# RG-LRU gates placed one by one among the products of a later projection, in a hybrid RG-LRU / latent-attention layer

## The chip, the core and the metric

The kernel runs on one core of a Trainium2 chip. TensorE (PE) multiplies matrices into PSUM, VectorE (DVE) and ScalarE (ACT) work on what it leaves there, GpSimd (POOL) takes elementwise work, and the queue of SyncE (SP) issues the DMAs. Each engine takes its instructions in order and waits at an instruction until the semaphores that it names are high enough. The metric is the device time in microseconds, as the median of several runs. Before the change it is 1305.29 us (three runs, 1304.16 to 1306.97).

## What is computed

One layer of a diffusion backbone: 1024 latent tokens and 256 context tokens of width 1024. This is the part of the reference that the change touches:

```python
xr_l, gr_l, cq_l, ckv_l, kr_l = split_in_proj(h_lat @ w_in)       # and the same for h_ctx
xcv_l = dwconv(xr_l, lru_conv_w, lru_conv_b, LRU_CONV_LEFT)        # 4 taps along the tokens
...
r = sigmoid(einsum('blhi,hij->blhj', xh, w_a) + b_a)               # 8 heads of 64
i = sigmoid(einsum('blhi,hij->blhj', xh, w_x) + b_x)
log_a = -LRU_C * r * softplus(-lam)
a = exp(log_a)
u = sqrt(-expm1(2 * log_a)) * (i * xc)                             # h_t = a_t h_(t-1) + u_t, both directions
...
y_lru_l = (lat_states[0] + lat_states[1]) * gelu(gr_l)
```

Beside it stand the modulation vectors silu(c) @ w_mod, the latent attention (its keys and values come from ckv), the output projection and a gated convolutional FFN.

## The kernel before

The program has five parts, one behind the other: a first part that loads and normalises the tokens and projects the token-major columns; the eight feature-major projections, with the RG-LRU between them; the start of the attention (values, keys, queries); the attention; the output projection and the FFN. The change is in the second part alone.

There, `proj` makes one block of 128 columns of `w_in` at a time. Every product is done as three fp32r products (high x high, high x low, low x high), over eight slices k of the contraction, into one PSUM tile with the tag "big" (name pf). Blocks 0 to 3 are the inputs of the convolution and cover all 1280 tokens (72 products), blocks 4 to 7 are the gelu branch and cover 1024 (48 products). `conv(m, po)` has ScalarE copy the block out of PSUM twice, VectorE adds the taps, and two DMAs write the halves of 64 rows, exchanged, into a page of their own (`xcs`). `gate(m, d, g)` makes one of the four gates of block m (two directions, a and x) from `xc` and `xcs`: six fp32 products in 64x64 tiles of the array, into another "big" tile (name pg), and a sigmoid on ScalarE that empties it. The tag "big" has two buffers, which the projections and the gates share; a product into a third tile waits until one of the two has been read. `coefs` (Exp, Tanh and the product with xc) and `scans` (Sqrt, then two scans in each direction on VectorE) follow. The table `after = {1: 0, 2: 1, 3: 2, 5: 3}` says behind which projection the four gates, coefs and scans of block m are written; for block 3 `tok_norm` and `ckv_t` (ten transposes of ckv into tiles with the tag "sm", names ck) come behind its coefs, and its scans one projection later.

The sixteen modulation steps (`mod2_step`) also stand between the projections, three or two at a time. Each takes two pages of `w_mod` (512 KB each, DMAs on SyncE's queue) and issues four fp32 products of 32 columns, two for each page (j) and half (h), each in its own quarter of the array, into a tile with the tag "sm" (name pm). Every fourth step ends a vector: ScalarE copies it out, and four small products or one wide one bring it into its place (the last goes through VectorE and two small DMAs for each half of the row). The tag "sm" has two buffers as well, shared by pm and ck. The pages of `R()` are twelve, used by w_mod, xr, xc, xcs, gates and coefficients in turn.

Inside the second part a scheduler of the framework sets the order of each engine's instructions, from the order in which the program is written and from an estimate of when operands are ready; `tc.issue_after(x)` holds what is issued inside its block behind x. The first part, the attention and the FFN are ordered by hand; the scheduler also orders the start of the attention.

Of the kernel before, what the change touches and what calls it, by code (L numbers as in the profile page):

```python
# [34 lines left out]
def hybrid_layer_kernel(ctx: ExitStack, tc: tile.TileContext, A, out):  # L35
# [20 lines left out]
    def R(dt=F32, shape=(128, 1280)):  # L56
        cnt[0] += 1
        return rp.tile(list(shape), dt, tag="R", name=f"r{cnt[0]}")
# [343 lines left out]
    acc2 = {}  # L402
# [10 lines left out]
    def mod2_step(s):  # L413

        n, kp = divmod(s, 4)
        if s + 1 < 16:
            mod2_load(s + 1)
        if kp == 0:
            acc2[n] = ps_small()
        ws_ = w2.pop(s)  # L420
        for j in range(2):
            for h in range(2):
                g = 64 * h + 32 * j
                T.matmul(acc2[n][g:g + 32, :], cs[:, 2 * kp + j, :], ws_[j][:, h * 512:(h + 1) * 512], start=kp == 0, stop=kp == 3,
                         tile_position=(0, g))
        if kp == 3:
            mr = R()
            S.activation(mr[:, 0:512], acc2.pop(n), AF.Copy)
            po = ps_small()
            if n < 2:  # L430
                pt = po[:, 0:8].rearrange("p (m h) -> p m h", h=2)
                for m in range(4):
                    T.matmul(pt[:, m, :], mr[:, m * 128:(m + 1) * 128], sel2, start=True, stop=True)
                V.tensor_copy(mod2[:, n].rearrange("p (h m) -> p m h", h=2), pt)
            else:
                T.matmul(po[0:2, :], sel2, mr[:, 0:512], start=True, stop=True)
                r = 2 * (n - 2)
                rw, gr = (mr[0:2, 512 + 256 * x:768 + 256 * x] for x in range(2))
                for h in range(2):
                    c = slice(h * 256, (h + 1) * 256)  # L440
                    for x, q_ in ((rw, r), (gr, r + 1)):
                        nc.sync.dma_start(out=x, in_=A["rows"][q_:q_ + 1, :].rearrange("o (a b) -> (o a) b", a=2)[:, c])
                    V.tensor_tensor(rw, po[0:2, c], rw, ALU.add)
                    V.tensor_tensor(rw, rw, gr, ALU.mult)
                    nc.sync.dma_start(out=gt_d[n - 2:n - 1, :].rearrange("o (a b) -> (o a) b", a=2)[:, c], in_=rw)
# [36 lines left out]
        split(raw, hi, lw, eh, el)  # L482
        return hi, lw

    def proj(w, chunks, name):

        hi, lw = w
        po = ps1.tile([128, 1536], F32, tag="big", name=name, bufs=2)
        for k in range(8):
# [4 lines left out]
                T.matmul(po[:, t0:t0 + n], wh, h_rng(hlo, k, t0, n), start=False, stop=False)  # L494
            for t0, n in chunks:
                T.matmul(po[:, t0:t0 + n], wl, h_rng(hhi, k, t0, n), start=False, stop=(k == 7))
        return po


# [33 lines left out]
    def conv(m, po):  # L533
# [9 lines left out]
                V.scalar_tensor_tensor(out=x[:, a:b], in0=xr[:, a + d:b + d], scalar=cw[k], in1=x[:, a:b],  # L543
                                       op0=ALU.mult, op1=ALU.add)

        y = xcs[m] = R()
        for p in (0, 64):
            nc.sync.dma_start(out=y[64 - p:128 - p, :], in_=x[p:p + 64, :])

# [22 lines left out]
        S.activation(g[:, :SEQ], po[:, :SEQ], AF.Gelu_apprx_tanh)  # L572
        V.tensor_tensor(ysum[m], ysum[m], g[:, :SEQ], ALU.mult)

    def gates(m):
        return [(gate(m, d, 0), gate(m, d, 1)) for d in range(2)]

    def coefs(m, ri):

        au = []  # L580
        for d in range(2):
            r, i = ri[d]
            c = slice(d * 4 + m, d * 4 + m + 1)
            a = R()
            S.activation(a, r, AF.Exp, scale=n8[:, c])
# [83 lines left out]
        return ps1.tile([128, 512], F32, tag="sm", name=f"pm{cnt[0]}", bufs=2)  # L669

    order = list(range(8))
    after = {1: 0, 2: 1, 3: 2, 5: 3}
    ws = prep_w(load_w(A["w_fm"][0]), "a", "v")
    raw = load_w(A["w_fm"][1])
    STEPS2 = [range(3 * n, 3 * n + 3) if n < 4 else range(12 + 2 * (n - 4), 14 + 2 * (n - 4)) if n < 6 else () for n in range(8)]
    with tc.issue_after(last_x.ins), tc.issue_after(last_h.ins):
        mod2_load(0)
    for n, m in enumerate(order):
        po = proj(ws, CH3 if m < 4 else CH3[:2], f"pf{m}")
        if n < 7:  # L680
            ws = prep_w(raw, "a", "v")
            if n < 6:
# [5 lines left out]
            conv(m, po)  # L688
        else:
            gated(m - 4, po)  # L690
        if m in after:
            au = coefs(after[m], gates(after[m]))
            if m == 5:
                tok_norm()
                ckv_t()
                au3 = au
            else:
                scans(after[m], au)
        if m == 6:
            raw = load_w(A["w_ukv"])  # L700
            wkh, wkl = prep_w(raw, "a", "v")
            scans(3, au3)
    pe_ctx.close()
    pe_ctx = ExitStack()
    ps2 = pe_ctx.enter_context(tc.tile_pool(name="ps2", bufs=4, space=PSUM, reuse_waits="tile"))
# [1072 lines left out]
```

## Time and profile before

| what | value |
|---|---|
| median of three runs | 1305.29 us (1304.16 to 1306.97) |
| the profiled execution | 1307.54 us |
| its span, first to last instruction | 1305.7 us |
| busy: PE / DVE / ACT / POOL | 97% / 78% / 56% / 30% |
| PE idle, all waits together | about 40 us of the span |
| second part (the projections) on PE | 90 to 247 us |
| mean granted clock of TensorE | 0.99 |

A busy share is an average over the whole span. The chain of waits follows the last instruction back to what released it, step by step; a share of it is time that set the end. In a timeline a row gives the start, the duration, the engine, the source line, the operation, and what it writes and reads; in brackets stands how long the engine was idle before it and who released it. Line numbers in these rows are those of the kernel before.

### The profile page before, as it was taken

The numbers are of one execution on the slowest core, as the hardware profiler recorded it, in microseconds if no ns is written. First come the engines' busy times: TensorE is split into PE (matmuls) and PEld (weight loads), VectorE is DVE, ScalarE is ACT, GpSimd is POOL, SyncE is SP. The second block draws the span as 40 slices with busy tenths as digits, with TensorE's granted clock in tenths as the row PEclk, the third lists the DMA queues.
The fourth block names the chain that finished last, engine by engine and source line by source line (L and its number), as shares of the span: only waits on it lengthen the run. The fifth ranks groups of instructions, "written<-read, shape, count | busy, mean of one in ns | idle before, by whom it ended". The sixth has DMA issues, their size and how long they took to land.

```text
span 1305.7 us, 18162 instructions
## 1 busy us (share of the span) xinstructions
PE 1265.6 (97%) x6586; PEld 1042.3 (80%) x6586; DVE 1012.0 (78%) x1665; ACT 735.5 (56%) x1376; POOL 388.9 (30%) x366
## 2 busy tenths in 40 slices
PE   5999999899999999999998999999999999999997
PEld 2796665687999999888877888888888888888886
DVE  3653677767888888857579888777877878897798
ACT  4543885557999999953375334433442343434581
POOL 2410000225666666733100443244234320000013
PEclk9999999999999999999998999999999999999999
DMA  9534463000000001243422222221222149205043
GB/s 371 206 102 149 128 193 124 13 1 2 2 1 2 2 1 30 86 162 113 146 80 97 83 83 77 97 97 67 79 97 81 66 141 365 90 1 177 1 146 129
DMA packets 45737, 126.85 MB, mean 97 GB/s; under 512 B 9016, under 2 KB 9296, under 8 KB 45648
## 3 DMA queue, kind: packets, MB, share of 16 engines
q1 hardware_dynamic: 45648, 125.69, 27.9%
q8 instruction: 52, 0.85, 0.3%
q14 instruction: 37, 0.30, 0.1%
HBM read 101.02 MB, written 22.03 MB: 94 GB/s over the span
## 4 chain that ended last, share of the span: by engine, by line
PE 81%; DVE 10%; ACT 4%; DMA 3%; issue 2%; SPq 0%; DVEq 0%; POOL 0%; ACTq 0%; POOLq 0%
PE b L1240 10%; PE b L1238 10%; PE b L1239 10%; PE t L937 5%; PE po L1086 4%; PE b L1415 4%; PE b L1416 4%; PE b L1414 4%; PE o L961 3%; PE o L962 3%; PE s L901 3%; PE s L902 3%; PE s L903 3%; DVE l L76 2%; PE po L1089 2%; PE pf L492 2%
## 5 line engine op out<-in xcount | busy, mean ns | idle before, releaser
L1240 PE MATMUL b<-l,f 128*128 128x512 f32 x620 | 242.6, 391 | 2.2 <-DVE f L76 2.2
L1238 PE MATMUL b<-l,f 128*128 128x512 f32 x620 | 242.5, 391 | 1.9 <-ACT f L1213 1.4
L1239 PE MATMUL b<-l,f 128*128 128x512 f32 x620 | 242.4, 391 | 0.9 <-DVE l L76 0.9
L1240 PEld LDWEIGHTS b<-l,f 128*128 128x128 f32 x620 | 117.1, 189 | 27.2 <-DVE f L76 3.0
L1238 PEld LDWEIGHTS b<-l,f 128*128 128x128 f32 x620 | 117.1, 189 | 26.7 <-ACT f L1213 1.9
L1239 PEld LDWEIGHTS b<-l,f 128*128 128x128 f32 x620 | 117.0, 189 | 26.1 <-DVE l L76 1.7
L1213 ACT ACTIVATE f<-w 128x1024 fp32r<-128x1024 f32 x21 | 22.3, 1060 | 201.9 <-POOL w L1210 193.6
L929 POOL TENSOR_SCALAR r<-r,c 128x512 f32<-128x512 f32 (+1 forms) x128 | 100.8, 799 | 97.9 <-DVE c L924 55.0
L906 DVE TENSOR_REDUCE c<-s 128x1 f32<-128x512 f32 (+1 forms) x192 | 108.7, 594 | 26.1 <-PE s L903 24.5
L76 DVE TENSOR_TENSOR f<-w,f 128x1024 fp32r<-128x1024 f32 (+1 forms) x90 | 98.4, 1095 | 34.1 <-ACT f L1213 33.1
L1297 DVE SCALAR_TENSOR_TENSOR l<-f,c,l 128x1023 f32<-128x1023 f32 x88 | 121.5, 1381 | 0.7
L917 ACT ACTIVATE r<-s,c 128x512 f32<-128x512 f32 (+1 forms) x192 | 117.5, 620 | 6.3 <-DVE c L924 4.8
L1207 POOL TENSOR_TENSOR w<-w 128x512 f32<-128x512 f32 x19 | 24.5, 1288 | 300.9 <-DVE f L76 300.9
L76 DVE TENSOR_TENSOR l<-t,l 128x512 fp32r<-128x512 f32 x128 | 81.5, 679 | 1.5 <-ACT l L69 1.3
L937 PE MATMUL t<-c,r 128*128 128x128 f32 x640 | 81.7, 273 | 0.9 <-DVE r L76 0.6
L69 ACT ACTIVATE l<-t 128x512 fp32r<-128x512 f32 x128 | 69.4, 595 | 8.8 <-PE t L937 7.9
L937 PEld LDWEIGHTS t<-c,r 128*128 128x128 f32 x640 | 71.3, 140 | 2.6 <-PE t L937 0.8
L1291 ACT ACTIVATE l<-f,c 128x1024 f32<-128x1024 f32 x44 | 54.4, 1237 | 31.7 <-DVE f L1278 31.2
L1637 POOL TENSOR_TENSOR f<-f,w 128x1024 f32<-128x1024 f32 (+1 forms) x5 | 11.7, 2376 | 202.7 <-ACT l L1603 202.7
L901 PE MATMUL s<-r,w 96*128 96x512 f32 (+1 forms) x192 | 69.5, 362 | 1.0 <-ACT r L917 0.7
L1086 PE MATMUL po<-l,r 128*128 128x512 f32 x256 | 69.3, 390 | 0.0
L961 PE MATMUL o<-l,r 128*128 128x256 f32 x256 | 69.0, 303 | 0.0
(355 smaller groups left out, 3183.6 us busy)
## 6 DMA issues: line engine op xcount, KB each, us to landing
w<-in_w_up SPq DMA_DIRECT2D x44, 512.0 KB, 4.1
r<-in_w_mod SPq DMA_DIRECT2D x32, 512.0 KB, 6.7
act<-l SPq DMA_DIRECT2D x22, 512.0 KB, 2.9
l<-in_w_m SPq DMA_DIRECT2D x16, 512.0 KB, 9.8
l<-act SPq DMA_DIRECT2D x27, 256.0 KB, 5.1
l<-in_w_dn SPq DMA_DIRECT2D x27, 256.0 KB, 5.7
w<-in_w_fm SPq DMA_DIRECT2D x8, 512.0 KB, 3.4
w<-in_w_out SPq DMA_DIRECT2D x8, 512.0 KB, 3.4
```

The lines of the kernel that those rows point to most:

```text
L76: return (V if e == "v" else G).tensor_tensor(o, src, f(hi), ALU.subtract)
L901: T.matmul(ps[:, :n], qh[0:96, q], kh[0:96, a:a + n], start=True, stop=False)
L906: V.tensor_reduce(out=stat[:, i % 4, c:c + 1], in_=sc[i, c][:, :CK[c][1]], op=ALU.min, axis=AX.X)
L917: S.activation(pt_[i][:, a:a + n], sc.pop((i, c))[:, :n], AF.Exp, scale=-1.0, bias=st[:, 3:4], accum_out=st[:, 4 + c:5 + c])
L929: G.tensor_scalar(out=p[:, a:a + n], in0=p[:, a:a + n], scalar1=stat[:, i % 4, 7:8], scalar2=1.0, op0=ALU.mult, op1=ALU.mult)
L937: T.transpose(ps[:, c, :], pt_[i][:, (c0 + c) * 128:(c0 + c + 1) * 128], ident)
L961: T.matmul(OT[j], v, hi, start=(c == 0), stop=False)
L1086: T.matmul(po[:, n * 512:(n + 1) * 512], w, wo[k][0][:, n * 512:(n + 1) * 512], start=st, stop=en)
L1238: T.matmul(po, wh, bh, start=k == 0 and b == wb[0][1], stop=False)
L1239: T.matmul(po, wh, bl, start=False, stop=False)
L1240: T.matmul(po, wl, bh, start=False, stop=k == 3 and b == wb[-1][1])
L1297: V.scalar_tensor_tensor(out=x[:, a], in0=x0[:, b], scalar=P("fcw", j * 3 + k, 1), in1=x[:, a], op0=ALU.mult, op1=ALU.add)
```

## The change

Three things are edited. (1) `proj` takes a list `between`; behind the products of slice k it calls what stands at place k. For projections 2 to 5 these are, behind slices 1 to 4, the four gates of blocks 0 to 3, one each, then `coefs` behind the last gate, and behind slice 5 the scans (for block 3: `tok_norm` and `ckv_t`). The table `after` and the calls behind the projection go. The gates of blocks 0, 1 and 2, which stood behind projections 1, 2 and 3, are now written inside projections 2, 3 and 4, and those of block 3, which stood behind projection 5, inside it; in each case the projection's own PSUM tile is open meanwhile. (2) The page `xcs` is now the page `xr` itself: the exchanged halves overwrite the source of the convolution. (3) In a modulation step the first product issued is that of j = 1, h = 0, and the other three are held behind it by `issue_after`.

```diff
@@ -418,11 +418,14 @@
         if kp == 0:
             acc2[n] = ps_small()
         ws_ = w2.pop(s)
-        for j in range(2):
-            for h in range(2):
-                g = 64 * h + 32 * j
-                T.matmul(acc2[n][g:g + 32, :], cs[:, 2 * kp + j, :], ws_[j][:, h * 512:(h + 1) * 512], start=kp == 0, stop=kp == 3,
-                         tile_position=(0, g))
+        with ExitStack() as rest:
+            for j in (1, 0):
+                for h in range(2):
+                    g = 64 * h + 32 * j
+                    i = T.matmul(acc2[n][g:g + 32, :], cs[:, 2 * kp + j, :], ws_[j][:, h * 512:(h + 1) * 512], start=kp == 0,
+                                 stop=kp == 3, tile_position=(0, g))
+                    if (j, h) == (1, 0):
+                        rest.enter_context(tc.issue_after(i.ins))
         if kp == 3:
             mr = R()
             S.activation(mr[:, 0:512], acc2.pop(n), AF.Copy)
@@ -482,7 +485,7 @@
         split(raw, hi, lw, eh, el)
         return hi, lw
 
-    def proj(w, chunks, name):
+    def proj(w, chunks, name, between=()):
 
         hi, lw = w
         po = ps1.tile([128, 1536], F32, tag="big", name=name, bufs=2)
@@ -494,6 +497,8 @@
                 T.matmul(po[:, t0:t0 + n], wh, h_rng(hlo, k, t0, n), start=False, stop=False)
             for t0, n in chunks:
                 T.matmul(po[:, t0:t0 + n], wl, h_rng(hhi, k, t0, n), start=False, stop=(k == 7))
+            for s_ in between[k] if k < len(between) else ():
+                s_()
         return po
 
 
@@ -543,7 +548,7 @@
                 V.scalar_tensor_tensor(out=x[:, a:b], in0=xr[:, a + d:b + d], scalar=cw[k], in1=x[:, a:b],
                                        op0=ALU.mult, op1=ALU.add)
 
-        y = xcs[m] = R()
+        y = xcs[m] = xr
         for p in (0, 64):
             nc.sync.dma_start(out=y[64 - p:128 - p, :], in_=x[p:p + 64, :])
 
@@ -572,14 +577,16 @@
         S.activation(g[:, :SEQ], po[:, :SEQ], AF.Gelu_apprx_tanh)
         V.tensor_tensor(ysum[m], ysum[m], g[:, :SEQ], ALU.mult)
 
-    def gates(m):
-        return [(gate(m, d, 0), gate(m, d, 1)) for d in range(2)]
+    ri_ = {}
+
+    def gate_step(m, d, g):
+        ri_.setdefault(m, {})[d, g] = gate(m, d, g)
 
     def coefs(m, ri):
 
         au = []
         for d in range(2):
-            r, i = ri[d]
+            r, i = ri[d, 0], ri[d, 1]
             c = slice(d * 4 + m, d * 4 + m + 1)
             a = R()
             S.activation(a, r, AF.Exp, scale=n8[:, c])
@@ -669,14 +676,34 @@
         return ps1.tile([128, 512], F32, tag="sm", name=f"pm{cnt[0]}", bufs=2)
 
     order = list(range(8))
-    after = {1: 0, 2: 1, 3: 2, 5: 3}
+    inside = {2: 0, 3: 1, 4: 2, 5: 3}
+    au_ = {}
+
+    def coef_step(m):
+        au_[m] = coefs(m, ri_.pop(m))
+
+    def late(m):
+        if m == 3:
+            tok_norm()
+            ckv_t()
+        else:
+            scans(m, au_[m])
+
+    def between(n):
+
+        if n not in inside:
+            return ()
+        m = inside[n]
+        g = [lambda d=d, x=x: gate_step(m, d, x) for d in range(2) for x in range(2)]
+        return ((), (g[0],), (g[1],), (g[2],), (g[3], lambda: coef_step(m)), (lambda: late(m),))
+
     ws = prep_w(load_w(A["w_fm"][0]), "a", "v")
     raw = load_w(A["w_fm"][1])
     STEPS2 = [range(3 * n, 3 * n + 3) if n < 4 else range(12 + 2 * (n - 4), 14 + 2 * (n - 4)) if n < 6 else () for n in range(8)]
     with tc.issue_after(last_x.ins), tc.issue_after(last_h.ins):
         mod2_load(0)
     for n, m in enumerate(order):
-        po = proj(ws, CH3 if m < 4 else CH3[:2], f"pf{m}")
+        po = proj(ws, CH3 if m < 4 else CH3[:2], f"pf{m}", between(n))
         if n < 7:
             ws = prep_w(raw, "a", "v")
             if n < 6:
@@ -688,18 +715,10 @@
             conv(m, po)
         else:
             gated(m - 4, po)
-        if m in after:
-            au = coefs(after[m], gates(after[m]))
-            if m == 5:
-                tok_norm()
-                ckv_t()
-                au3 = au
-            else:
-                scans(after[m], au)
         if m == 6:
             raw = load_w(A["w_ukv"])
             wkh, wkl = prep_w(raw, "a", "v")
-            scans(3, au3)
+            scans(3, au_[3])
     pe_ctx.close()
     pe_ctx = ExitStack()
     ps2 = pe_ctx.enter_context(tc.tile_pool(name="ps2", bufs=4, space=PSUM, reuse_waits="tile"))
```

The scheduler makes this of it. On PE, at the gates of block 2 (pg is a gate, pf a projection, pm a modulation step, ck a transpose of ckv; the number is the buffer's), the kernel before has, up to the first product of projection 4 (pf_1554):

```order
L558 MATMUL pg_1507<-r_1304,l_1289 64x512 x2
L558 MATMUL pg_1507<-r_1295,l_1289 64x512 x2
L558 MATMUL pg_1507<-r_1295,l_1289 64x256 x2
L424 MATMUL pm_1613<-r_1458,c_77 32x512
L424 MATMUL pm_1613<-r_1459,c_77 32x512 x2
L558 MATMUL pg_1516<-r_1304,l_1289 64x512 x2
L558 MATMUL pg_1516<-r_1295,l_1289 64x512 x2
L558 MATMUL pg_1516<-r_1295,l_1289 64x256 x2
L558 MATMUL pg_1525<-r_1304,l_1289 64x512 x2
L558 MATMUL pg_1525<-r_1295,l_1289 64x512 x2
L558 MATMUL pg_1525<-r_1295,l_1289 64x256 x2
L492 MATMUL pf_1554<-l_208,w_1436 128x512
```

and the changed kernel, up to the first product of projection 5 (pf_1625), the same gates:

```order
L563 MATMUL pg_1522<-r_1292,l_1287 64x512 x2
L563 MATMUL pg_1522<-r_1293,l_1287 64x512 x2
L563 MATMUL pg_1522<-r_1293,l_1287 64x256 x2
L563 MATMUL pg_1537<-r_1292,l_1287 64x512 x2
L563 MATMUL pg_1537<-r_1293,l_1287 64x512 x2
L563 MATMUL pg_1537<-r_1293,l_1287 64x256 x2
L664 MATMUL ck_1760<-c_72,l_543 128x128 x2
L664 MATMUL ck_1760<-c_72,l_614 128x128 x2
L563 MATMUL pg_1552<-r_1292,l_1287 64x512 x2
L563 MATMUL pg_1552<-r_1293,l_1287 64x512 x2
L563 MATMUL pg_1552<-r_1293,l_1287 64x256 x2
L495 MATMUL pf_1625<-l_208,w_1599 128x512
```

The gates of block 2 have moved from before projection 4 to behind its last product, not among its products, and ckv's first transposes have come among them. The four gates of block 0 and the first two of block 1 stand among the products of projections 2 and 3; the last two of block 1 stand behind projection 3, and those of block 3 behind projection 5. A projection is broken into at 16 places in all, by gates or modulation steps.

On ACT, from the gates of block 2 on, the kernel before has (pf_1554 is projection 4, whose gelu is the last row):

```order
L585 ACT_TABLE_LOAD
L585 ACTIVATE r_1534<-r_1505,c_851 128x1280
L585 ACTIVATE r_1538<-r_1523,c_851 128x1280
L586 ACTIVATE r_1505<-r_1505,c_852 128x1280
L586 ACTIVATE r_1523<-r_1523,c_852 128x1280
L593 ACT_TABLE_LOAD
L593 ACTIVATE r_1505<-r_1505 128x1280
L593 ACTIVATE r_1523<-r_1523 128x1280
L69 ACTIVATE w_1678<-w_1607 128x1024
L572 ACT_TABLE_LOAD
L572 ACTIVATE r_1626<-pf_1554 128x1024
```

and the changed kernel (its projection 4 is pf_1494):

```order
L570 ACTIVATE r_1544<-pg_1537,c_70 128x1280
L570 ACTIVATE r_1559<-pg_1552,c_70 128x1280
L592 ACT_TABLE_LOAD
L592 ACTIVATE r_1561<-r_1514,c_851 128x1280
L592 ACTIVATE r_1565<-r_1544,c_851 128x1280
L593 ACTIVATE r_1514<-r_1514,c_852 128x1280
L593 ACTIVATE r_1544<-r_1544,c_852 128x1280
L600 ACT_TABLE_LOAD
L600 ACTIVATE r_1514<-r_1514 128x1280
L600 ACTIVATE r_1544<-r_1544 128x1280
L577 ACT_TABLE_LOAD
L577 ACTIVATE r_1622<-pf_1494 128x1024
```

In both the gelu that empties projection 4's PSUM tile stands behind the coefficients and square roots of block 2; in the changed kernel the gates of block 2 are issued on PE between that projection and its gelu.

On DVE, at the reading of the first ckv tile, the kernel before has (ck_1811):

```order
L443 TENSOR_TENSOR r_1696<-pm_1698,r_1696 2x256
L76 TENSOR_TENSOR w_1880<-w_1682,w_1879 128x1024
L444 TENSOR_TENSOR r_1696<-r_1696 2x256
L587 TENSOR_TENSOR r_1729<-r_1729,r_1486 128x1280
L662 SCALAR_TENSOR_TENSOR l_1809<-ck_1811,c_70,l_1808 128x512
L443 TENSOR_TENSOR r_1696<-pm_1698,r_1696 2x256
L444 TENSOR_TENSOR r_1696<-r_1696 2x256
L587 TENSOR_TENSOR r_1747<-r_1747,r_1486 128x1280
L662 SCALAR_TENSOR_TENSOR l_1809<-ck_1818,c_70,l_1808 128x512
```

and the changed kernel (ck_1760):

```order
L608 SCALAR_TENSOR_TENSOR r_1529<-r_1561,r_1529 128x256
L612 SCALAR_TENSOR_TENSOR r_1559<-r_1565,r_1559 128x256
L609 SCALAR_TENSOR_TENSOR r_1529<-r_1561,r_1529 128x1024
L614 SCALAR_TENSOR_TENSOR r_1559<-r_1565,r_1559 128x1024
L578 TENSOR_TENSOR l_1228<-l_1228,r_1622 128x1024
L618 TENSOR_TENSOR l_1585<-r_1529,r_1559 128x1024
L651 COPY l_1720<-l_506 128x2x32
L627 TENSOR_TENSOR l_1720<-c_855,c_856 128x2x32
L669 SCALAR_TENSOR_TENSOR l_1758<-ck_1760,c_70,l_1757 128x512
L623 TENSOR_TENSOR c_855<-l_614,c_74 128x64
```

The read of the first ckv tile (the last row; in the kernel before the fifth) has moved from among the products with xc of block 3 to behind the scans of block 2 (the rows of 256 and 1024 columns) and their sum.

## Rows read from the trace of the kernel before

**Rows 1.** The page: busy us of each engine, share of the span, instructions.
```profile
PE 1265.6 (97%) x6586; PEld 1042.3 (80%) x6586; DVE 1012.0 (78%) x1665; ACT 735.5 (56%) x1376; POOL 388.9 (30%) x366
```
**Rows 2.** Windows between two projections: length, then busy PE, PEld, DVE, ACT, POOL.
```profile
174.26:185.87 11.61, 11.47 (x75) 3.10 (x74) 11.61 (x12) 8.87 (x9) 0.00 (x0) 1.00 0.41 114
197.02:200.85 3.83, 2.03 (x9) 0.29 (x8) 3.83 (x4) 3.54 (x4) 0.00 (x0) 1.00 0.87 334
...
sum 50.82, PE 48.02 PEld 14.98 DVE 40.48 ACT 39.21 POOL 0.00; mean PE 9.60 PEld 3.00 DVE 8.10 ACT 7.84 POOL 0.00
```
**Rows 3.** Chain of waits around projection 1: start, duration, what.
```profile
107.10 0.78 PE pf L492 x3
107.88 0.58 PE pf L494 x3
...
121.37 1.00 PE pm L424 x8
122.37 1.00 PE pg L558 x2
...
126.79 1.83 PE pm L424 x10
```
**Rows 4.** Chain of waits: the last gate of block 1 and projection 3.
```profile
157.12 1.48 PE pg L558 x12
...
158.62 1.34 ACT r L565
...
160.00 0.85 PE pf L492 x3
```
**Rows 5.** Timeline of ACT behind the gates of block 2.
```profile
187.13 1.28 ACT L585 ACT_TABLE_LOAD   x1
```
**Rows 6.** Timeline of DVE: modulation row, scans of block 2, ckv read, scans of block 3.
```profile
183.83 0.41 DVE L443 TENSOR_TENSOR r<-pm,r 2x256 f32<-2x256 f32 x1
...
189.92 0.41 DVE L443 TENSOR_TENSOR r<-pm,r 2x256 f32<-2x256 f32 x1 [0.46 <-DMA r<-in_rows]
...
196.18 2.89 DVE L598 SCALAR_TENSOR_TENSOR r<-r,r 128x1280 f32<-128x1280 f32 x2 [2.60 <-ACT r L593]
...
208.58 1.21 DVE L611 TENSOR_TENSOR l<-r,r 128x1024 f32<-128x1024 f32 x1
...
223.31 0.74 DVE L662 SCALAR_TENSOR_TENSOR l<-ck,c,l 128x512 fp32r<-128x512 f32 x1
...
234.88 1.49 DVE L598 SCALAR_TENSOR_TENSOR r<-r,r 128x1280 f32<-128x1280 f32 x1 [1.80 <-ACT r L593]
```
**Rows 7.** Timeline of PE: the wait for a page of w_mod.
```profile
199.87 1.05 PE L424 MATMUL pm<-r,c 128*32 128x512 f32 x4 [1.80 <-DMA r<-in_w_mod]
```
**Rows 8.** Windows there and later: busy as above, then the granted clock.
```profile
198.00:200.00 2.00, 0.20 (x4) 0.13 (x4) 2.00 (x2) 1.97 (x3) 0.00 (x0) 1.00 1.02 410
...
202.00:204.00 2.00, 2.00 (x6) 1.53 (x5) 2.00 (x3) 0.00 (x0) 0.00 (x0) 0.50 0.77 219
...
272.00:276.00 4.00, 3.75 (x21) 3.78 (x22) 3.09 (x10) 2.76 (x8) 1.65 (x4) 1.00 0.02 4
```
**Rows 9.** Chain of waits: projection 5 behind that wait, and behind the last projection.
```profile
203.36 0.85 PE pf L492 x2
...
205.46 0.46 PE pf L492 x2
...
245.29 1.98 DVE r L598
...
258.02 0.43 PE pb L737
```
**Rows 10.** Timeline of PE from the end of the last projection on.
```profile
246.93 1.91 PE L722 MATMUL pb<-c,l 128*128 128x128 f32 x16
...
257.23 0.79 PE L736 MATMUL pb<-w,l 128*128 128x512 f32 x1 [5.66 <-DVE l L725]
...
272.25 0.41 PE L774 MATMUL pb<-l,l 128*128 128x384 f32 x1 [1.06 <-DVE r L805]
```

## The prediction

> **What bounds the kernel now.** I read the page first: PE is busy for 97% of the span, the next engine for 78% [rows 1]. Up to projection 0 and from the values on, the first work behind projection 7, nothing is edited and each engine's order is the same as before, so a shift of the first attention product reaches the end one for one. The question is how long PE takes from projection 1 to that product. Windows come next: the five stretches between projections, in which the gates and the modulation steps stand, take 50.82 us, and PE is busy in 48.02 of them [rows 2]. There is little idle time there to win: 1.80 us for a page of w_mod [rows 7], the rest in parts under a microsecond. The larger wait stands behind the last projection, 5.66 us for VectorE's L725 [rows 10], which comes behind the scans of block 3.
>
> **What PE's own work loses.** In the kernel before, a gate whose first product or first three stand alone costs a second piece, since a lone product takes as long as four beside each other: 1.00 us for one product, 1.00 for the four of a modulation step [rows 3]. Of the sixteen gates four are broken so, by my count of the order. The modulation steps of the five stretches come in groups that take 17 such times (five products count as two, 1.83 [rows 3]); in the changed kernel there are 15. So 4 + 2 = 6 us go. Against that a projection is now broken into at 16 places, and the first three products behind such a place take 0.78 instead of 0.58 us [rows 3]: 16 x 0.19 = 3.0. Sum: -3.0 us. Products that are kept together cost nothing more, since the page that they wait for last is the same.
>
> **What PE waits for instead.** Projections and gates share two PSUM tiles. In the kernel before, projection m's tile is emptied before or during the gates, and these alternate between two tiles: a gate hides the sigmoid of the one before. In the changed kernel the open projection holds one tile through all its gates, and in the case of projections 4 and 5 until its gelu, which stands on ACT behind the sigmoids, exponentials and square roots of the gates. So each gate waits for the sigmoid of the gate before. What such a round trip costs shows where the kernel before has one: the last gate of block 1 starts at 157.12, its sigmoid at 158.62, the projection that needs a tile at 160.00 [rows 4]. That is 2.88 us, 1.48 of it the gate's: 1.40 of waiting, unless something else stands between. Among the products of projections 2 and 3 something does, and I cost those gates at nothing (if ACT were late there, 1.40 each, six of them). Behind the projections nothing does:
> Block 1: third to fourth gate, fourth gate to projection 4, 2 x 1.40 = 2.8.
> Block 2: first to second gate 0.4 (a lone modulation product of 1.00 stands between), then 3 x 1.40 = 4.6. The first ckv transposes, between its third and fourth gate, take a small PSUM tile that VectorE frees with the second half of a modulation row. In the kernel before, the two halves are 6.09 us apart [rows 6]. Counted from the start of projection 4, the first half comes after ACT's coefficients (9.05 us, from 187.13 to 196.18 [rows 5, 6]) and the scans of block 1 (13.61 to the end of the row at 208.58, less about 2.3 for the two sums there: 11.3), the second at 26.8. PE gets there after 11.15 for the projection (185.87 to 197.02 [rows 2]), three insertions of 1.2, then 1.0, 1.45, 1.0, 0.4, 1.45, 1.4 and 1.45: 22.9. So 4.0 instead of 1.40, 2.6 more (bounds 0 and 4.5).
> Block 3: again 0.4. Then the second ckv group waits for VectorE to have read the first, and that read stands behind the scans of block 2. From the last sigmoid of block 2: 9.05 + 13.61 + 1.0 for three small rows (0.74 is the read itself [rows 6]) = 23.7 us. PE is there after 11.15 + 1.2 + 1.0 + 1.45 + 1.0 + 0.4 + 1.45 = 17.6. Wait: 6.1 (bounds 1.4, were the read ahead of the scans, and 8). The third ckv group waits in the same way for about 1.6, the last gate's sigmoid for 1.4. Sum 9.5.
> Together 2.8 + 4.6 + 2.6 + 9.5 = 19.5 us.
>
> **What goes.** The waits of the five stretches, 50.82 - 48.02 = 2.8 us [rows 2]. The exchanged halves in the page of xr free one page per block of twelve, which lets loads start earlier, but their DMAs still wait for the last tap; I take nothing for it (bounds: 1.8 won or lost, the size of that wait [rows 7]). With the wait goes the slow stretch behind it: pairs of products take 0.85 us there and 0.46 after it [rows 9], five pairs, 1.8 us. Sum: -4.6.
>
> **The clock.** Behind a stretch of 2.00 us with PE busy in 0.20, the granted clock was 0.50, which is 1.2 of 2.4 GHz; behind a wait of 1.06 us it stayed at 1.00 [rows 8, 10]. The changed kernel has three stretches in which PE waits for a third to a half of the time. Nearest is the row above, so I take one such slow stretch of 1.8 us behind each: +5.4. Bounds: nothing, and all ten of those gates at half the clock beside it, 10 x 1.45 = 14.5 more.
> The Trainium skill speaks against the change here ("TensorE: Matmul & The Clock Gate", section "A second HAM failure mode: psum-queue depth-cycling"): where TensorE idles briefly but often between groups of products because it cycles through PSUM tiles, the clock swings between its two levels. By it the sum would go to the upper bound; no row here shows a wait for a PSUM tile that repeats, so it is a rival below.
>
> **The end of the stretch.** Before: 5.66 us of waiting [rows 10] and then twelve products at 0.43 [rows 9] instead of 0.23 (half a pair's 0.46), 2.4: 8.1. After: from the last sigmoid of block 3, ACT takes 9.05; VectorE's scans, sums and L725 took 22.3 from 234.88 [rows 6] to 257.19, just before PE goes on, and get two pairs of small rows more, 23.4 in all, 2.1 of which are stretched rows such as L598's 1.98 us (1.49 at 234.88) [rows 6, 9]. That is 30.3 to 32.4. PE needs 2 x 11.15, two insertions of 1.2 and the 4.6 us from 246.93 to where the wait began [rows 10]: 29.3. So a wait of 1.0 to 3.1, taken as 2, and 1 for the clock (0 to 2.4). Change: 3 - 8.1 = -5.1.
>
> **Sum.** -3.0 + 19.5 - 4.6 + 5.4 - 5.1 = +12.2 us. Against the profiled execution, 1307.54 (span 1305.7 and 1.8 around it), that is 1319.7; that execution is 2.25 above the median of 1305.29, so the median comes to 1317.5. About 0.2%, 2.6 us, is what a measurement of this kernel can tell from no change.
>
> **Rivals.**
> Shorter waits (chance 0.18): the clock stays full through the three stretches and VectorE's tail is not stretched. For it: a wait of 1.06 us left the clock alone. Against: a wait of 6.1 us is among the new ones, longer than the 5.66 that did lower it. 12.2 - 5.4 - 3 = +3.8, 1309.
> Gates at half the clock (0.15): the upper bound above, +12.2 + 14.5 = +26.7, 1332; also w_mod pages that come late inside a projection would show as such a time.
> The waits don't come, faster (0.09): one mechanism, the second PSUM tile. If a projection's tile is read out before its gates need it, the gates alternate as before, and of the 19.5 us nothing is left but the ckv waits that the scans no longer force. Then -3.0 - 4.6 = -7.6, with the wait for L725 kept: 1298. It is decided by whether the gelu of projections 4 and 5 comes ahead of their gates' sigmoids on ACT. Against: in the order it stands behind the square roots.
> No change (0.04): the change does not do what it says. For blocks 2 and 3 it doesn't, since their gates are behind a projection and not among its products; if their waits are then no more than today's waits and the tail gives back the rest, the time stays at 1305.
>
> **How the numbers follow.** The forecast has a chance of 0.54 and a range of its own of 1311 to 1325. The time is its 1317.5. The range reaches down to the shorter waits, 1308, and up to 1330, short of the far end of the half clock. Faster 0.08, same 0.06 (the no-change case and the low end of the short waits), slower 0.86.
>
> **What would show it.** In the changed profile the gates behind projections 3, 4 and 5 should wait for the sigmoid (ACT, line of `gate`) for about 1.4 us each, the second ckv group for VectorE's ckv read for about 6 us, and projections 4, 5 and 6 for the last sigmoid before them; PE's wait for L725's counterpart should fall from 5.66 to under 3. The attention should start 10 to 15 us later, relative to projection 1, and be as long as before. I am wrong if PE's waits between projections 1 and 7 come to under 10 us, if the gates behind a projection alternate between two tiles, or if the attention changes in length.

## The result, and the profile after

The changed kernel takes 1317.66 us (median of four runs, 1317.13 to 1318.62); the kernel before took 1306.13 in the same session (1304.16 to 1307.28). The ratio is 1.0091, with a 95% interval of 1.0073 to 1.0108: slower by 11.5 us. The profiled execution took 1318.62 us, its span is 1316.8, 11.1 more than before.

The page's busy line of the changed kernel (busy us, share, instructions), against [rows 1]:

```profile
PE 1265.5 (96%) x6586; PEld 1040.0 (79%) x6586; DVE 1007.3 (76%) x1665; ACT 735.8 (56%) x1376; POOL 386.2 (29%) x366
```

PE is as busy as before to a tenth of a microsecond and the span is 11 us longer. Two windows show where. The first goes from the start of the projection that the prediction calls 0 to the end of the last one, the second from there to the first attention product. First the kernel before, then the changed one; the columns are length, busy PE, PEld, DVE, ACT, POOL, then the granted clock of TensorE (1.00 is full speed):

```profile
90.15:247.09 156.94, 154.08 (x833) 100.70 (x833) 102.38 (x132) 97.13 (x88) 8.11 (x5) 0.99 0.45 138
247.09:285.76 38.67, 31.61 (x174) 27.70 (x171) 30.42 (x39) 17.98 (x34) 8.50 (x10) 0.91 0.00 1
```

```profile
90.68:265.44 174.76, 155.96 (x833) 99.04 (x833) 103.04 (x135) 97.40 (x88) 0.63 (x1) 0.96 0.39 121
265.44:296.66 31.22, 29.04 (x173) 25.80 (x171) 25.52 (x36) 17.98 (x34) 13.29 (x13) 1.00 0.06 22
```

The same 833 products take 17.8 us longer, 15.9 of it waiting (174.76 - 155.96 = 18.80 against 2.86) and 1.9 of it busy time; the stretch behind the last projection is 7.5 shorter, at a clock of 1.00 instead of 0.91. With 0.5 for the later start the attention begins 10.9 us later (296.66 against 285.76). That is the span's 11.1 within 0.2: it kept its length.

PE's waits in the first of the two windows of the changed kernel (line, releaser, us in total, times, longest). Where [rows 7] stood, a wait for w_mod, there is none. In the second window the wait of [rows 10] (here for L744) is 0.81 us instead of 5.66; its row is shown further down:

```profile
PE ck L664 <- DVE r L446: 5.6, 1, 5.6
PE pg L563 <- ACT r L570: 4.7, 5, 1.4
PE pf L495 <- ACT r L570: 4.3, 3, 1.4
PE ck L664 <- DVE l L669: 4.2, 1, 4.2
```

The timeline of PE (start, duration, what, idle time before) has them one by one; the first three rows answer to [rows 4], and each sequence ends in the first product of the next projection:

```profile
169.44 1.52 PE L563 MATMUL pg<-r,l 64*64 64x512 f32 x12
172.39 1.52 PE L563 MATMUL pg<-r,l 64*64 64x512 f32 x12 [1.43 <-ACT r L570]
175.34 0.73 PE L495 MATMUL pf<-l,w 128*128 128x512 f32 x2 [1.43 <-ACT r L570]
...
196.94 1.52 PE L563 MATMUL pg<-r,l 64*64 64x512 f32 x12 [1.43 <-ACT r L570]
204.04 1.11 PE L664 MATMUL ck<-c,l 128*128 128x128 f32 x4 [5.58 <-DVE r L446]
205.08 2.84 PE L563 MATMUL pg<-r,l 64*64 64x512 f32 x12
209.35 1.22 PE L495 MATMUL pf<-l,w 128*128 128x512 f32 x2 [1.43 <-ACT r L570]
...
227.21 1.52 PE L563 MATMUL pg<-r,l 64*64 64x512 f32 x12 [0.45 <-ACT r L570]
232.93 0.89 PE L664 MATMUL ck<-c,l 128*128 128x128 f32 x4 [4.20 <-DVE l L669]
233.74 2.83 PE L563 MATMUL pg<-r,l 64*64 64x512 f32 x12
238.00 1.52 PE L563 MATMUL pg<-r,l 64*64 64x512 f32 x12 [0.97 <-ACT r L570]
240.95 0.72 PE L495 MATMUL pf<-l,w 128*128 128x512 f32 x2 [1.43 <-ACT r L570]
```

A gate now starts 2.95 us after the one before it (172.39 - 169.44), 1.52 of it the gate's products and 1.43 waiting, close to the 2.88 of [rows 4]. The four gates of block 0 and the first two of block 1, which stand among products, wait for nothing. Behind each of the two long waits one gate takes 2.84 or 2.83 instead of 1.52, at about half the clock (windows further down). On DVE (timeline as in [rows 6]) these are the two halves of the modulation row, the second of which ends the first long wait, and the first ckv read, which ends the second:

```profile
195.63 0.39 DVE L446 TENSOR_TENSOR r<-pm,r 2x256 f32<-2x256 f32 x1
...
203.58 0.41 DVE L446 TENSOR_TENSOR r<-pm,r 2x256 f32<-2x256 f32 x1
...
232.13 0.74 DVE L669 SCALAR_TENSOR_TENSOR l<-ck,c,l 128x512 fp32r<-128x512 f32 x1
```

### The profile page after: what moved, and what is told of

It reads as the page before. It is cut to its first block, busy times and chain, and to the rows that moved or that the text cites. A ratio compares the mean times of both kernels' runs of the same rounds, so it can differ in the third digit from the quotient of the medians.

```text
span 1316.8 us, 18162 instructions
## 1 busy us (share of the span) xinstructions
PE 1265.5 (96%) x6586; PEld 1040.0 (79%) x6586; DVE 1007.3 (76%) x1665; ACT 735.8 (56%) x1376; POOL 386.2 (29%) x366
## 4 chain that ended last, share of the span: by engine, by line
PE 79%; DVE 12%; ACT 5%; issue 2%; DMA 1%; SPq 0%; DVEq 0%; ACTq 0%; POOL 0%; POOLq 0%
PE b L1259 10%; PE b L1257 10%; PE b L1258 10%; PE t L956 5%; PE po L1105 4%; PE b L1434 4%; PE b L1435 4%; PE b L1433 4%; PE o L980 3%; PE o L981 3%; PE s L920 3%; PE s L921 3%; PE s L922 2%; DVE l L76 2%; PE po L1108 2%
```

## The experiments

Times are medians; a ratio, with its 95% interval, is to the kernel before, run on the same chip beside it. The medians of the kernel before in these sessions lie between 1305.77 and 1306.75 us, so a difference between two runs of different sessions is uncertain by about 1 us. The three parts of the change are called gates, page and steps, in the order in which the change names them.

**Gates alone.** The changed kernel, with parts 2 and 3 taken back:

```diff
-        with ExitStack() as rest:
-            for j in (1, 0):
...
-                        rest.enter_context(tc.issue_after(i.ins))
+        for j in range(2):
...
-        y = xcs[m] = xr
+        y = xcs[m] = R()
```

> Only the gates are moved, as in the changed kernel; the exchanged halves have a page of their own and the modulation steps are issued as before. Theory (gates behind a projection wait for a sigmoid because they share one free PSUM tile with it, and the ckv transposes for VectorE; the page costs and gives nothing, keeping the steps together gives about 2 us): PE's waits between projections 1 and 7 as in the changed kernel, about 19 us, time 2 us above it, 1319 to 1321 us. Rival (the page matters: without it the pages of w_mod and of the gates come free later): waits for DMA or pages beside those, 1325 us or more. Rival (the page or the steps are what costs): 1308 or less.

Measured: 1335.21 us (four runs, 1334.48 to 1337.98), ratio 1.0229 [1.0214, 1.0243]. The gates alone cost 29 us, 17.5 more than the whole change, and the theory, by which page and steps were worth only 2 us, falls. The time is in the range of the rival that the page matters, but its sign, waits for DMA, is not there. PE's largest waits:

```profile
PE pg L560 <- ACT r L567: 9.4, 7, 2.2
PE ck L661 <- DVE r L443: 6.5, 1, 6.5
PE pf L492 <- ACT r L567: 4.7, 4, 1.4
PE ck L661 <- DVE l L666: 4.6, 1, 4.6
```

These are 25.2 instead of 18.8, and the projections take 193 us (90.92 to 283.97), 18.3 more than in the changed kernel. More of that is work than waiting: PE is busy for 166.90 us instead of 155.96, the modulation steps taking 24.9 instead of 18.7 and the gates 31.0 instead of 27.0. The order differs too: a modulation step is cut in two halves, with projection products between them.

**Page and steps, without the gates.** The kernel before, with parts 2 and 3:

```diff
-        for j in range(2):
+        with ExitStack() as rest:
+            for j in (1, 0):
...
+                        rest.enter_context(tc.issue_after(i.ins))
...
-        y = xcs[m] = R()
+        y = xcs[m] = xr
```

> The exchanged halves in the page of the source and the steps kept together, with the gates behind the projections as before. Theory: no waits for sigmoids beyond those of before, the steps 2 us shorter, 1303 to 1305 us. Rival (page or steps are what costs): 1312 us or more. Rival (keeping the steps together makes PE wait for the later of two pages of w_mod): 1306 to 1310 us, with PE waiting for w_mod by more than before's 1.8 us.

Measured: 1308.2 us (11 runs, 1306.95 to 1308.91), ratio 1.0017 [1.0008, 1.0026]. The timeline of PE between projections 3 and 4 shows it waiting twice for w_mod, 2.8 us together:

```profile
179.13 1.07 PE L425 MATMUL pm<-r,c 128*32 128x512 f32 x8 [1.82 <-DMA r<-in_w_mod]
...
183.43 1.93 PE L425 MATMUL pm<-r,c 128*32 128x512 f32 x6 [0.96 <-DMA r<-in_w_mod]
```

By themselves the two parts win nothing and cost some 2 us (1 to 3 by the interval). The rival's time and sign hold, its reason only in part: PE is idle for 5.7 us of the projections instead of 2.9, and w_mod has 1.0 of the difference; a wait for VectorE's half row (0.9) and one for ScalarE's copy of a modulation vector (0.7) are new as well. What the parts are worth depends on the gates; the next two runs take them apart.

**Gates and steps, page of its own.**

```diff
-        y = xcs[m] = xr
+        y = xcs[m] = R()
```

> Gates moved as in the change and a modulation step's products kept together; the exchanged halves keep a page of their own. The gates alone took 1335.2 us, 17.5 more than the changed kernel. Theory (steps): without the kept-together products a modulation step is split in two halves among the products of a projection, each of which takes the 1.00 us of a whole one; by the order, the products in groups of up to four take 28 such times with the gates alone, 22 in the changed kernel, 23 here. So nearly all comes back: 1317 to 1322, and all modulation groups have one, three or four products. Rival (page): the page of its own delays the loads of w_mod and with them the steps: 1330 to 1337, with waits for w_mod or late gates. Half and half would be 1325 to 1329.

Measured: 1331.02 us (four runs, 1330.04 to 1331.21), ratio 1.0194 [1.018, 1.0209]. Only four of the 17.5 us come back, where the theory had nearly all; the time is in the rival's range, with late gates and without a wait for w_mod. The largest wait:

```profile
PE ck L664 <- DVE r L446: 10.3, 1, 10.3
```

and the second gate of block 1 on PE's timeline:

```profile
171.16 2.83 PE L563 MATMUL pg<-r,l 64*64 64x512 f32 x12 [2.22 <-ACT r L570]
```

Only block 1's first gate stands among projection 3's products and three behind it; in the changed kernel two and two. The second waits 2.22 us although products stand ahead of it: ScalarE has a weight copy and a table load to do first, so the first gate's sigmoid starts at 169.78, 3.3 us after that gate's products. Of block 0 three instead of four gates stand inside. And in block 2 the first transposes come ahead of three of the gates instead of one, so PE comes early to a tile that VectorE frees late: 10.3 instead of 5.6.

**Gates and page, steps as before.**

```diff
-        with ExitStack() as rest:
-            for j in (1, 0):
...
-                        rest.enter_context(tc.issue_after(i.ins))
+        for j in range(2):
```

> Gates moved as in the change and the exchanged halves in the page of xr; the modulation step issued in its old way. Theory (steps): the order still holds the split steps (27 group times, 28 with the gates alone), so the time stays near that of the gates alone: 1330 to 1337. Rival (page): the page is what the gates alone lacked: 1316 to 1321. Half and half: 1325 to 1329.

Measured: 1322.96 us (four runs, 1320.7 to 1325.59), ratio 1.0135 [1.0117, 1.0153]. That is between the two theories' ranges. So both parts count, the page for more: it brings 12.3 us without the steps kept together (1335.21 to 1322.96) and 13.4 with them (1331.02 to 1317.66); the steps bring 4.2 without the page and 5.3 with it. A saving of that size shows in the products: by lines, the modulation steps' 128 products take 23.9 us here (line L424) and 18.7 in the changed kernel (L425). The columns are busy us, mean ns of one, and idle time before; first this kernel, then the changed one:

```profile
L424 PE MATMUL pm<-r,c 128*32 128x512 f32 x128 | 23.9, 603 | 0.0
```

```profile
L425 PE MATMUL pm<-r,c 128*32 128x512 f32 x128 | 18.7, 603 | 0.0
```

It is not all that differs. Between the two profiled executions the projections differ by 7.1 us (181.90 against 174.76): beside the 5.2 of the steps, the projections' own products take 4.2 and the gates 0.8 us longer here, at a granted clock of 0.93 instead of 0.96, and the waits are 3.1 shorter. This profiled execution is 2.6 us above the median of its kernel, so the 5.3 can't be split among these terms.

The page's part shows as order: with it block 0's fourth gate and block 1's second stand among the products again, and only one gate of block 2 stands behind the first transposes. Whether the page has an effect beyond the order was not separated.

**The ckv transposes later.** The changed kernel, with `tok_norm` and `ckv_t` behind projection 6:

```diff
-        return ((), (g[0],), (g[1],), (g[2],), (g[3], lambda: coef_step(m)), (lambda: late(m),))
+        return ((), (g[0],), (g[1],), (g[2],), (g[3], lambda: coef_step(m)), (lambda: late(m),) if m < 3 else ())
...
         if m == 6:
...
+            late(3)
```

> The changed kernel with the token norms and the ckv transposes written behind projection 6 and not behind slice 5 of projection 5. Theory: the two waits of ckv's transposes (5.6 and 4.2 us) go, the gates beside which they stood wait 1.4 us for a sigmoid instead, at three places: 5 to 7 us less, 1311 to 1313 us. Rival (the round trips through the sigmoid and the clock make the loss, the ckv waits only cover them): within 2 us of the changed kernel, 1316 to 1319. Rival (the transposes then come late for the values): 1316 or more with a wait of the values.

Measured: 1312.39 us (four runs, 1312.08 to 1313.43), ratio 1.0052 [1.0037, 1.0067], as the theory had it: 5.3 us less than the changed kernel. The two windows of this kernel, and PE's waits:

```profile
90.94:256.67 165.73, 151.24 (x833) 96.76 (x832) 102.99 (x135) 97.55 (x88) 1.34 (x2) 1.00 0.43 131
256.67:291.12 34.45, 30.63 (x174) 26.93 (x171) 27.26 (x36) 17.99 (x34) 14.77 (x13) 0.95 0.00 1
```

```profile
PE pg L563 <- ACT r L570: 8.0, 7, 1.4
PE pf L495 <- ACT r L570: 4.3, 3, 1.4
PE pb L756 <- DVE l L745: 2.4, 1, 2.4
```

Without the two long waits the ten round trips cost 12.3 us and the clock is 1.00 from the first projection to the last: no slow stretch. So the slow stretches of the changed kernel hang on the waits of 5.58 and 4.20 us. The projections are 9.0 us shorter than in the changed kernel; 3.2 of that is given back behind them (34.45 against 31.22), where the wait for VectorE is 2.42 instead of 0.81, with a slow clock behind it.

**Blocks 2 and 3 as before.** The changed kernel, with only blocks 0 and 1 among the products:

```diff
-    inside = {2: 0, 3: 1, 4: 2, 5: 3}
+    inside = {2: 0, 3: 1}
+    behind = {3: 2, 5: 3}
```

> The changed kernel, with the gates of blocks 2 and 3 written behind projections 3 and 5 as before, those of blocks 0 and 1 among the products of projections 2 and 3. Theory (the open projection holds one of the two large PSUM tiles; the waits come from the gates that stand behind their projection): the waits of blocks 2 and 3 for a sigmoid and those of ckv's transposes go, those of block 1 (2.8 us) stay; the wait behind the last projection comes back in part. 1308 to 1313. Rival (each place at which a projection is broken into costs, in clock or in weight loads, and not the waits): half of the 11.5 us goes with half of the places, and no more: the waits fall but the time stays at 1311 to 1316 with slow stretches of the clock inside projections 2 and 3. Rival (no part of the loss hangs on blocks 2 and 3): 1316 to 1319.

Measured: 1316.67 us (four runs, 1314.98 to 1317.09), ratio 1.0082 [1.0066, 1.0098]. The waits:

```profile
PE pm L425 <- DMA r<-in_w_mod: 7.2, 4, 3.4
PE pb L762 <- DVE l L751: 5.6, 1, 5.6
PE pg L563 <- DMA r<-r: 2.3, 2, 1.9
```

The waits for sigmoids and transposes are gone but for 2.0 us, as the theory says, and the time is not: PE waits 7.2 us for pages of w_mod and 2.3 for the exchanged halves of block 2, and the 5.6 behind the last projection is back in full. The time is in the second rival's range and just above the first's, but neither reason holds: the clock is slow from 176 to 191 us, among the steps and gates behind projection 3, and from 214 to 220, and not inside projections 2 and 3. The late loads show on SyncE's queue: it stands for 10.7 us at the copies of block 2's exchanged halves, which wait for VectorE's taps and are issued at 171.35, and issues the next six loads of w_mod behind them, from 173.54 on. Which page each of these loads waited for is open. Since other waits came in the place of those that went, this run does not settle what the gates of blocks 2 and 3 cost.

**Block 3 earlier.** A version of another kind: the kernel before, with the steps kept together, the gates of block 3 behind projection 4, its scans and ckv's part behind projection 5.

```diff
-    after = {1: 0, 2: 1, 3: 2, 5: 3}
+    inside = {}
+    behind = {1: 0, 2: 1, 3: 2, 4: 3}
...
+        if m == 5:
+            tok_norm()
+            ckv_t()
...
-            scans(3, au3)
+        if m == 5:
+            scans(3, au_[3])
```

> The kernel before with the steps kept together and with the gates, coefficients and scans of block 3 behind projection 4 and 5 instead of 5 and 6 (ckv behind projection 5). Theory: the gates alternate between two PSUM tiles as before, VectorE's scans of block 3 end some 11 us earlier, so the wait of 5.66 us behind the last projection and the slow clock after it (2.4 us) go, and the steps are 2 us shorter: 1295 to 1299 us. Rival (the twelve pages hold it back: block 3's pages come free no earlier, so the wait only moves into projections 4 and 5): 1303 to 1307 us.

Measured: 1297.04 us (five runs, 1296.82 to 1300.01), ratio 0.9937 [0.9925, 0.995]: 8.8 us less than the kernel before, as the theory had it, and faster than the changed kernel too. Its two windows:

```profile
89.98:244.89 154.91, 150.02 (x833) 98.65 (x833) 105.73 (x136) 94.84 (x86) 6.81 (x5) 0.99 0.45 141
244.89:275.05 30.16, 28.73 (x173) 25.91 (x171) 22.95 (x34) 18.00 (x34) 6.71 (x9) 1.00 0.00 1
```

The profiled executions differ by 10.5 us: 8.5 of it behind the last projection (30.16 against 38.67), 2.0 before. The longest wait left in the projections is one for w_mod:

```profile
PE pm L425 <- DMA r<-in_w_mod: 3.2, 2, 2.7
```

**The same with the old steps.** The version above, with:

```diff
-        with ExitStack() as rest:
-            for j in (1, 0):
...
-                        rest.enter_context(tc.issue_after(i.ins))
+        for j in range(2):
```

> The kernel before with one edit: the gates of block 3 behind projection 4 and its scans behind projection 5, with ckv's part; modulation steps issued as before. Against the earlier run that also kept a step's products together (1297.0). Theory (the gain is that of the earlier scans alone, 5.7 us of waiting and the slow clock behind it, and the kept-together steps gave nothing or cost up to 2 us as they did with the page): 1294 to 1299, same as or faster than that run. Rival (the kept-together steps bring part of it, by fewer groups of products): 1299 to 1303.

Measured: 1298.77 us (five runs, 1297.73 to 1299.18), ratio 0.9947 [0.9934, 0.996]. The intervals of the two overlap, and the time is in the theory's range. The early block 3 is the gain; what the steps add is no more than about the 1.7 us between the medians. Keeping the products together saves time here too, 17.3 us for the steps' products instead of 21.4, but part of it goes in waits: PE is idle for 4.9 us of the projections instead of 3.0.

The one long wait for w_mod here is 1.90 us, and no slow stretch follows it: the clock is 1.00 from the first projection to the last.

```profile
200.84 1.05 PE L424 MATMUL pm<-r,c 128*32 128x512 f32 x4 [1.90 <-DMA r<-in_w_mod]
```

```profile
91.08:247.16 156.08, 153.13 (x833) 99.04 (x832) 105.83 (x136) 95.07 (x86) 6.80 (x5) 1.00 0.45 139
```

**Scans of block 3 where they were.** Block 3 earlier with the steps kept together, and:

```diff
-        if m == 5:
+        if m == 6:
             scans(3, au_[3])
```

> The fastest version so far (1297.0: gates of block 3 behind projection 4, a modulation step's products kept together, scans of block 3 and ckv's part behind projection 5) with one edit: the scans of block 3 stand behind projection 6 again, as in the kernel before. Theory (the gain needs only the early gates: from the last sigmoid of block 3 to the first attention product there are then one projection more than before for the coefficients and scans; VectorE is not the last to arrive either way): 1295 to 1299, no wait for the normalised input of the values (L725 of before) behind the last projection. Rival (the scans themselves must stand early, since behind projection 6 VectorE's other rows come first): the wait behind the last projection comes back, by 2 to 5 us, and with it the slow clock: 1300 to 1305.

Measured: 1296.57 us (five runs, 1295.63 to 1297.3), ratio 0.9923 [0.9909, 0.9936], and no wait for the values' input, as the theory had it. So the early gates are enough. It and the version with early scans are the fastest here and are not told apart.

## Why the prediction was right

The forecast of 1317.5 us came to 1317.66, its +12.2 to +11.1 in the span, by the mechanism named but with terms that err in both directions. That the median fits to 0.2 us is luck: the span's change was put 1.1 too high, and 2.25 was taken off for the distance from a profiled execution to the median, which is 0.96 in the changed kernel. Point by point, with the two windows as the measure: projections +17.3 predicted (-3.0 + 19.5 - 4.6 + 5.4), +17.8 measured; the end -5.1 predicted, -7.5 measured. The start of projection 0, 0.5 later, stands in no term.

**PE's own work, -3.0: about -1.** The kernel with ckv later shows it, since its clock is full: 151.24 us of busy PE, against 154.08 less 1.8 for the slow stretch before. By lines in that window, first the kernel before, then that one:

```profile
L492 PE MATMUL pf<-l,w 128*128 128x512 f32 x160 | 45.0, 378 | 0.4
...
L496 PE MATMUL pf<-l,w 128*128 128x512 f32 x160 | 44.1, 373 | 0.0
L558 PE MATMUL pg<-r,l 64*64 64x512 f32 (+1 forms) x192 | 27.4, 531 | 0.0
L424 PE MATMUL pm<-r,c 128*32 128x512 f32 x128 | 20.2, 601 | 1.8 <-DMA r<-in_w_mod 1.8
```

```profile
L495 PE MATMUL pf<-l,w 128*128 128x512 f32 x160 | 45.5, 377 | 4.3 <-ACT r L570 4.3
...
L499 PE MATMUL pf<-l,w 128*128 128x512 f32 x160 | 45.1, 375 | 1.1 <-DVE w L76 1.1
L563 PE MATMUL pg<-r,l 64*64 64x512 f32 (+1 forms) x192 | 24.3, 535 | 8.0 <-ACT r L570 8.0
...
```

The gates lost 3.1 (4 predicted), the steps 1.5 (20.2 to 18.7; 2 predicted). The projections (three lines each, the first and the last shown), 133.6 less the 1.8, came to 135.9: 4.1 for the places at which they are broken into, not 3.0, or about 0.25 at each (16 places, and one more by the transposes in that kernel).

**What goes, -4.6: about that.** The waits of before, 2.86, and the slow stretch behind the one for w_mod are gone. (Five pairs at 0.85 instead of 0.46 would be 1.95, not the 1.8 of the sum; by their starts in the trace the five take 0.60, three times 0.85 and 0.82, 1.7 more than at full clock.)

**Waits, 19.5: 18.80.** The price of a round trip was read from the wrong gate. The row at 157.12 in [rows 4] is block 1's third gate in the kernel before, not its last; PE's timeline has two gates of twelve there:

```profile
157.05 2.81 PE L558 MATMUL pg<-r,l 64*64 64x512 f32 x24
```

The fourth gate ran while the third's sigmoid did, and projection 3 started at 160.00, right behind it: PE hardly waited. The 2.88 is a gate and its sigmoid all the same, and where nothing stands between, as in the changed kernel, the wait came to 1.43 (1.40 predicted). The six gates among products, taken at nothing, waited for nothing. Block 1 has 2.86 (2.8 predicted). Block 2 has 0.45 + 1.43 + 5.58 + 1.43 = 8.9 (7.2). The wait at the transposes was 1.6 longer than the 4.0: VectorE's second half row came 7.95 us behind the first, not 6.09, with a sum (L618, 1.20) and a product with xc (L594, 1.47) between them. Block 3 has 0.45 + 4.20 + 0.97 + 1.43 = 7.05 (9.5). VectorE read the ckv tile 23.5 us behind the last sigmoid of block 2, as worked out (23.7). PE came there after 19.4 instead of 17.6: the first products of projection 5 ran at half the clock (1.22 and 1.05 us a pair instead of 0.62). The sum adds the time that the slow clock takes to the path, beside a wait of 6.1. In the run the 1.8 us came out of that wait, which was 4.20. And the third transposes didn't wait at all: the gate ahead of them, 2.83 at half the clock, covered it. That is the step of the sum that failed in kind: clock and wait were added where they overlap.

**The clock, +5.4: +4.7**, by the difference in busy time to the kernel with ckv later (155.96 - 151.24). The size fits, the parts do not: there are two slow stretches, at the two waits of over 4 us, and none in block 1, where three were taken; 2.7 of the 4.7 is in gates, which the sum left at full clock. Windows of the changed kernel, the first long wait, then the second and what follows it (granted clock third from the end):

```profile
198.46:204.04 5.58, 0.01 (x2) 0.00 (x1) 5.58 (x9) 1.33 (x1) 0.00 (x0) 0.86 0.23 52
...
228.73:233.00 4.27, 0.07 (x1) 0.08 (x2) 4.27 (x8) 1.33 (x1) 0.00 (x0) 1.00 0.00 0
233.00:236.00 3.00, 3.00 (x16) 1.18 (x16) 3.00 (x6) 0.69 (x1) 0.00 (x0) 0.53 0.00 0
```

In the second wait the clock is full to the end and half of it (1.2 of 2.4 GHz) in the work behind, as in [rows 8]; in the first it has fallen before the wait ends (0.86 over the wait). The rival of gates at half the clock is partly true: two gates of ten were. For all ten, the Trainium skill's "TensorE: Matmul & The Clock Gate" spoke (section "A second HAM failure mode: psum-queue depth-cycling": short repeated idling over PSUM tiles makes the clock swing). The kernel with ckv later bears on it: ten such waits, 12.3 us in all and none over 1.43, at a granted clock of 1.00. There the trace does not agree. But where the clock was low already, it stayed low through such waits: with the gates alone, a wait of 2.22 in block 1 is followed by two gates at half the clock, with waits of 1.42 and 1.43 before them. The second:

```profile
181.44 2.84 PE L560 MATMUL pg<-r,l 64*64 64x512 f32 x12 [1.43 <-ACT r L567]
```

**The end, -5.1: -7.5.** The wait is 0.81 instead of 2, and the twelve products behind it run at full clock. PE came after 29.0 us (29.3 worked out), VectorE after 29.8, below the 30.3 to 32.4 of the prediction: its row L605 took 1.50 and 1.47 us, where L598, the same row before, was stretched to 1.98 [rows 9].

```profile
270.73 0.50 PE L755 MATMUL pb<-w,l 128*128 128x512 f32 x1 [0.81 <-DVE l L744]
```

**What was costed at nothing.** The page was given no price, and the kept-together steps only the 2 us of fewer groups, both in the order of the whole change. For the whole change that holds, since their effect was in that order. Taken apart, page and steps are worth 17.5 us to a kernel whose gates are inside; without that they cost 2. The parts do not add.

**The rivals.** Shorter waits needed a full clock through the projections, which was not so here. Waits that don't come and no change needed gates that alternate between two tiles or wait no longer than before; the rows show neither.

## What to carry to other kernels

Where the open block holds one of two PSUM tiles, pieces of work that follow one another all go through the other tile, and each waits for the reader of the one before: 2.95 us for a gate of 1.52. Six gates of sixteen were hidden all the same, since enough products stood between them; so look at the order that the scheduler makes, not at the place in the program. (A third tile was not tried.) Before moving work, look for the wait that ends the stretch: moving block 3's gates one projection up gave 8.5 us behind the last projection, at the price of a wait for w_mod of 2.7 (4.4 with the later scans). When waits and a slow clock follow each other on one engine, work them out in order of time, since a delay ahead of a wait is taken out of the wait.

## What was not expected

Keeping a modulation step's four products together saves 5 us of product time, since a half step takes the time of a whole one (1.06 us on PE's timeline for two products and for four): 128 products took 18.7 us in one order, 23.9 in the other. What of it shows in the time differs: 4 to 5 us with the gates inside, about 1.7 at most with block 3 early, where PE waits longer for w_mod. And ten waits of at most 1.43 us left the clock at 1.00, while single waits of 1.80 [rows 7, 8], 2.22, 2.42, 4.20 and 5.58 us each had a slow stretch at or behind them; one of 1.90 had none. What decides between 1.80 and 1.90 the runs do not show.
